# Moving the matmul operands of a two-layer encoder kernel to other SBUF addresses, with three more warming products

## The chip, the cores and the metric

The kernel runs on one core of a Trainium2 chip. The metric is the device time of one execution in microseconds. Before the change three runs gave 1088.2, 1091.89 and 1095.99 us, so the median is 1091.89 us. All times of single instructions below come from one profiled execution of its own.

## What is computed

The reference is a two-layer streaming encoder in float32, on 512 frames of width 1024. Cut to what matters here, one layer is:

```python
h = rms(x, norm1); z = h @ w_in            # 1024 -> 2572 columns, three groups of heads
x = x + concat(swa(z), fox(z), mlstm(z)) @ w_out      # 1024 -> 1024
u = rms(x, norm2) @ w_ff1                  # "first matrix", 1024 -> 4096
x = x + square(relu(u)) @ w_ff2            # "second matrix", 4096 -> 1024
```

`swa` is sliding-window attention with sinks and rotary positions, `fox` is attention with a forgetting bias, and `mlstm` is a chunkwise matrix memory. The change touches only the two products of the feed-forward part, `w_ff1` and `w_ff2`, and the first microseconds of the program.

## The kernel before

**Three products for one.** Every large matmul is done on float32r operands that are split into a high and a low part: `mm3` (lines 260 to 263) issues high times high (L261), high weight times low operand (L262) and low weight times high operand (L263), all three added in one PSUM bank. ScalarE rounds a weight tile to its high part `whi` (L203), VectorE subtracts to get the low part `wlo` (L204). Both are 128 x 1024 tiles with three buffers each. Weights arrive in `raw` and `fraw` tiles by DMA.

**Which side is loaded.** In the input projection (`big_work`, lines 516 to 552) the activations `xhl` are the stationary operand, loaded into the array 128 columns at a time, and `whi`/`wlo` stream through, 256 or 268 columns wide. In the output projection (L553 to L572) and in the feed-forward part the weights are stationary, and the activations stream: `yg` 512 columns wide in the output projection, `xhl` 512 columns wide in the first eight steps of the feed-forward part, then everything 256 columns wide. TensorE runs a weight load for the next matmul while the present one streams (PEld beside PE in the profile).

**The feed-forward part** (lines 1071 to 1335). The first quarter of the first matrix is done plainly (`ff1_std`), the rest of it and all of the second matrix with seven products in place of eight for each 2 x 2 block of sub-matrices (`ff1_st`, `ff2`; the order of the seven is ORDER, line 47). The seven products need sums and differences of blocks:

- The sums of x for the first matrix lie in the tile `xbx` (8 x 1024 floats a partition): `xsums` writes them, `xop` picks them (lines 332 to 370).
- The operands of the second matrix are sums of squared activations, made in the tile `ct` and split by `gsplit` and `csplit` (lines 1146 to 1155) into *units* of 1024 floats, which is 4096 bytes a partition. A unit holds the high or the low part of a pair of blocks (in `csplit` both, one block each). There are fourteen units in a queue, `units` (lines 1084 and 1085): six in the tile `gx`, eight in the tile `ygx`, which held the attention's output `yA` before. They are handed out by `unit_for` and given back by `give`. Two more, `quads`, lie in `xhl` and join late.

**Order of the work.** The generators of the first and the second matrix alternate by hand: `ff_pairs` (lines 117 to 126) gives the order, `getjob`/`prep_ahead` split weights up to three jobs ahead (`HIB`), and `load_ahead` starts DMAs as soon as a `raw` or `fraw` buffer is free.

**Addresses.** Tiles of one phase come from a pool that is opened with `open_phase` and gets the byte addresses from its tags in order of first use. In the program as compiled, the byte address inside a partition, taken modulo 512, is:

| operand | first address | modulo 512 | role |
|---|---|---|---|
| `whi`, `wlo` (all buffers) | 108992 ... 129472 | 448 | stationary in the output projection and feed-forward part, streaming in the input projection |
| `xhA`, `xlA` in `xhl` | 30720 | 0 | stationary, input projection |
| `yA` in `ygx` | 63936 | 448 | streaming, output projection |
| `xh`, `xl` in `xhl` | 30592 | 384 | streaming, feed-forward part |
| `xbx` (sums of x) | 134528 | 384 | streaming, first matrix |
| units 0 to 5 in `gx` | 167296 + 4096 i | 384 | streaming, second matrix |
| units 0 to 7 in `ygx` | 63872 + 4096 i | 384 | streaming, second matrix |

Every slice that a matmul streams or loads starts a multiple of 512 bytes after the tile or unit, so the last column but one holds for all of them. Before, a 40-float tile `pad` at the start of the feed-forward pool moves `xbx` and `gx` from 224 to 384 modulo 512.

**The start of the program.** Eight products of the constant tile `ones_m` with itself (lines 290 and 291) run while the first DMAs are under way. Each is a plain float32 matmul and has two records in the profile.

Of the kernel before, what the change touches and what calls it, by code (L numbers as in the profile page):

```python
# [13 lines left out]
F32R = mybir.dt.float32r  # L14
# [5 lines left out]
P = 128  # L20
D = 1024
S = 512
# [6 lines left out]
EPS = 1e-6  # L29
WGAP = 32  # L30
YGAP = 16
SWA_Q = 512
THETA = 10000.0

# [16 lines left out]
def trunk(ctx, tc, x, cols, rows, gate_w, tabs, w_in, w_out, w1, w2, out):  # L51
# [5 lines left out]
    xpool = ctx.enter_context(tc.tile_pool(name="xpool", bufs=1))  # L57
# [7 lines left out]
    def nm(s):  # L65
        cnt[0] += 1
        return f"{s}_{cnt[0]}"

    ATT = {"ms": (S, 5), "zq": (640, 6), "zv": (260, 8), "tmp": (768, 3), "rowb": (S, 4), "scs": (S, 4),
           "qk": (2 * S, 5), "pT": (S, 4), "hs": (256, 2), "co": (256, 4)}  # L70
    FFP = {"pad": (40, 1), "xbx": (8 * D, 1), "gx": (6 * D, 1), "xt": (S, 2), "ct": (6 * S, 1), "fraw": (4 * D, 1),
           "ms": (S, 2)}
    phase = {}

    def open_phase(tags):
        stack = ExitStack()
        phase["stack"] = stack
        phase["tags"] = tags
        phase["pool"] = stack.enter_context(tc.tile_pool(name=nm("ph"), bufs=1))

    def close_phase():
        phase.pop("stack").close()
        phase.clear()

    def wt(tag, name):
        n, bufs = phase["tags"][tag]
        return phase["pool"].tile([P, n], F32, tag=tag, name=nm(name), bufs=bufs)

    def att():
        return atp.tile([P, S], F32, tag="at", name=nm("at"))  # L90
# [4 lines left out]
    def v3(a, d=HD):  # L95
        return a.rearrange("p (h d) -> p h d", d=d)
# [175 lines left out]
    gx = cst.tile([P, NT, 36], F32, name="gx")  # L272
# [5 lines left out]
    XS = KT * S  # L278
    xT = xpool.tile([P, KT, S], F32, name="xT")
    xhl = xpool.tile([P, 2 * XS + 4 * WGAP], F32R, name="xhl")  # L280
    ygx = xpool.tile([P, 16 * S + YGAP], F32R, name="yg")
    sq_acc = {}
    xhA, xlA = (v3(xhl[:, WGAP + i * XS:WGAP + (i + 1) * XS], S) for i in range(2))
    xh, xl = (v3(xhl[:, i * XS:(i + 1) * XS], S) for i in range(2))
    yA, yg = v3(ygx[:, YGAP:], S), v3(ygx[:, :16 * S], S)


    open_phase(ATT)
    wps = att()
    for _ in range(8):  # L290
        T.matmul(wps[:, :P], ones_m, ones_m, start=True, stop=True)
    NN = 2 * L * KT
    pcol = cst.tile([P, NN + 2 * L], F32, name="pcol")
# [38 lines left out]
    def xb(i, j, t=None):  # L332
        t = (xh if t is None else t).rearrange("p (k i) q -> p k i q", i=2)
        return t[:, :, i, j * 256:(j + 1) * 256]
# [109 lines left out]
    for l in range(L):  # L444
# [612 lines left out]
        ct, bt = 0, 0  # L1057
# [13 lines left out]
        close_phase()  # L1071
        open_phase(FFP)
        pos["ff"] = l
        wt("pad", "pad")
        xbt["x"] = wt("xbx", "xbx").bitcast(F32R)
        gxt = wt("gx", "gx").bitcast(F32R)
        ct = v3(wt("ct", "ct"), S)
        fr = wt("fraw", "fraw")
        free_ff.extend(fr[:, i * D:(i + 1) * D] for i in range(4))
# [1 line left out]

        def unit(a):
            return a.rearrange("p (a f) q -> p a f q", a=2)
        units = deque(unit(v3(gxt[:, i * D:(i + 1) * D], 256)) for i in range(6))
        units.extend(yg[:, 2 * i:2 * i + 2].rearrange("p a (f q) -> p a f q", f=2) for i in range(8))
        quads = [unit(xb(0, 1, t_)) for t_ in (xh, xl)]
        banks = deque(att() for _ in range(8))

# [258 lines left out]
def _layout(x, norm1, w_in, swa_q_norm, swa_k_norm, swa_sinks, fox_q_norm, fox_k_norm, fox_f_bias, mlstm_i_bias,  # L1347
# [13 lines left out]
    def heads(w):  # L1361
        return w.reshape(2, 4, HD, -1).transpose(1, 0, 2, 3).reshape(SWA_Q, -1)
    w_in = cc([np.stack([heads(w[:, :SWA_Q].T).T for w in w_in]), w_in[:, :, SWA_Q:]], 2)
    w_out = cc([np.stack([heads(w[:SWA_Q]) for w in w_out]), w_out[:, SWA_Q:]], 1)
    cb = [np.stack([w_in[l][:, g[1][0][0]:g[1][0][0] + 256] for g in GROUPS]) for l in range(L)]
# [29 lines left out]
```

## Time and profile before

| | us |
|---|---|
| runs of the kernel | 1088.2, 1091.89, 1095.99 |
| profiled execution, device time | 1083.42 |
| profiled execution, span from first to last instruction | 1081.7 |
| TensorE with a matmul in it | 1064.2 |
| TensorE with a weight load in it | 997.5 |
| VectorE busy | 923.0 |
| ScalarE busy | 625.2 |

The stages of the profiled execution follow each other on TensorE: input projection of layer 0 from 6 us, with the attention's small matmuls between its products, output projection to 225 us, the 512-wide steps of the feed-forward part to 271 us, its 256-wide steps to 544 us; then the same for layer 1, from 544 to 686, 760, 806 and 1081.7 us.

How to read it: a matmul's record lasts from its start to a modelled end, some 280 ns for 256 columns, and the next one starts long before that end. So neither the mean of a group nor the busy share tells what a matmul costs. What it costs is the distance between the starts of neighbours, called *spacing* here. It comes from a table of stretches: the length of a stretch in which PE is busy throughout, divided by the matmuls in it, after taking off those that had started before the stretch (about 280 ns of records divided by the spacing).

### The profile page before, as it was taken

The page shows a single profiled execution, that of the slowest core. Times are in us where ns is not written, and L with a number is a line of the kernel's source. Part 1 is how long each engine was busy: PE and PEld are TensorE (multiplying, and loading weights), DVE is VectorE, ACT ScalarE, POOL GpSimd, SP SyncE. Part 2 cuts the span into 40 slices and gives each one's busy share as a digit, 9 for nine tenths or more (in the row PEclk, how much of TensorE's full clock was granted, in tenths as well). Part 3 has the DMA queues.
Part 4 walks back from the last instruction along what each step waited for, and adds up shares of the span by engine and source line. Part 5 has one row for each costly group of instructions (what it writes and reads, how often), then busy time and mean ns, then how long its engine had stood idle before and what let it go on. Part 6 is the DMA issues. An engine that isn't in the chain of part 4 may idle for free.

```text
span 1081.7 us, 21133 instructions
## 1 busy us (share of the span) xinstructions
PE 1064.2 (98%) x8488; PEld 997.5 (92%) x8488; DVE 923.0 (85%) x1572; ACT 625.2 (58%) x1099; POOL 106.3 (10%) x154
## 2 busy tenths in 40 slices
PE   9999999999999999999999999999999999999998
PEld 8999987887999999999999999778789999999998
DVE  7696868899997988999967877778999889899996
ACT  6445655375666667566545466544766575666552
POOL 2030010103110010010001200101000100010100
PEclk9999999999999999999999999999999999999999
DMA  6522111245378587587334321113334865876862
GB/s 216 161 95 97 60 59 58 65 169 127 115 201 218 132 218 209 145 211 210 106 110 158 96 78 55 65 50 128 114 91 137 233 176 169 240 177 174 221 171 98
DMA packets 47346, 151.81 MB, mean 140 GB/s; under 512 B 5632, under 2 KB 8832, under 8 KB 47248
## 3 DMA queue, kind: packets, MB, share of 16 engines
q1 hardware_dynamic: 39184, 121.10, 32.9%
q0 software_dynamic: 8064, 29.36, 15.5%
q8 instruction: 66, 1.08, 0.4%
q14 instruction: 32, 0.26, 0.1%
HBM read 147.86 MB, written 2.13 MB: 139 GB/s over the span
## 4 chain that ended last, share of the span: by engine, by line
PE 65%; DVE 18%; DMA 7%; ACT 6%; issue 3%; SPq 0%; POOL 0%; DVEq 0%; ACTq 0%; POOLq 0%
PE at L261 19%; PE at L263 19%; PE at L262 19%; DVE wlo L204 5%; DMA raw<-in_w_dram 5%; DVE rt L703 2%; DMA fraw<-in_w_dram 2%; ACT whi L203 2%; DVE xT L1257 1%; DVE yg L1150 1%; PE at L876 1%; PE at L834 1%; PE at L859 1%; PE at L733 1%; PE at L788 1%
## 5 line engine op out<-in xcount | busy, mean ns | idle before, releaser
L203 ACT ACTIVATE whi<-raw 128x1024 fp32r<-128x1024 f32 (+1 forms) x144 | 150.8, 1047 | 132.8 <-PE at L262 90.2
L204 DVE TENSOR_TENSOR wlo<-raw,whi 128x1024 fp32r<-128x1024 f32 (+1 forms) x144 | 174.7, 1213 | 38.4 <-ACT whi L203 37.8
L261 PE MATMUL at<-whi,xhl 128*128 128x256 f32 (+1 forms) x640 | 183.9, 287 | 1.2 <-ACT whi L203 1.2
L261 PE MATMUL at<-yg,whi 128*128 128x256 f32 (+1 forms) x592 | 180.1, 308 | 0.1
L262 PE MATMUL at<-wlo,xhl 128*128 128x256 f32 (+1 forms) x640 | 179.9, 281 | 0.1
L263 PE MATMUL at<-whi,xhl 128*128 128x256 f32 (+1 forms) x640 | 179.6, 281 | 0.0
L263 PE MATMUL at<-yg,wlo 128*128 128x256 f32 (+1 forms) x592 | 178.8, 302 | 0.5 <-DVE wlo L204 0.5
L203 ACT ACTIVATE whi<-fraw 128x1024 fp32r<-128x1024 f32 x122 | 129.3, 1060 | 85.0 <-PE at L262 67.2
L262 PE MATMUL at<-yg,whi 128*128 128x256 f32 (+1 forms) x560 | 169.7, 303 | 0.0
L262 PE MATMUL at<-xhl,whi 128*128 128x256 f32 (+1 forms) x544 | 165.5, 304 | 0.0
L204 DVE TENSOR_TENSOR wlo<-fraw,whi 128x1024 fp32r<-128x1024 f32 x122 | 148.9, 1221 | 6.1 <-ACT whi L203 5.6
L261 PE MATMUL at<-xhl,whi 128*128 128x256 f32 (+1 forms) x480 | 148.6, 310 | 0.0
L263 PE MATMUL at<-xhl,wlo 128*128 128x256 f32 (+1 forms) x480 | 147.8, 308 | 0.0
L261 PEld LDWEIGHTS at<-whi,xhl 128*128 128x128 f32 x640 | 121.4, 190 | 2.6 <-ACT whi L203 1.5
L262 PEld LDWEIGHTS at<-wlo,xhl 128*128 128x128 f32 x640 | 121.4, 190 | 0.4 <-DVE wlo L204 0.4
L263 PEld LDWEIGHTS at<-whi,xhl 128*128 128x128 f32 x640 | 121.4, 190 | 0.2 <-DVE xhl L328 0.2
L263 PEld LDWEIGHTS at<-yg,wlo 128*128 128x128 f32 x592 | 111.1, 188 | 6.2 <-DVE wlo L204 0.9
L261 PEld LDWEIGHTS at<-yg,whi 128*128 128x128 f32 x592 | 111.3, 188 | 5.9 <-issue 1.7
L263 PE MATMUL at<-xbx,wlo 128*128 128x256 f32 x384 | 106.6, 278 | 4.1 <-DVE wlo L204 4.1
L262 PEld LDWEIGHTS at<-yg,whi 128*128 128x128 f32 x560 | 105.3, 188 | 4.2 <-DVE yg L988 0.5
L262 PEld LDWEIGHTS at<-xhl,whi 128*128 128x128 f32 x544 | 102.1, 188 | 6.3 <-issue 0.5
L261 PE MATMUL at<-xbx,whi 128*128 128x256 f32 x384 | 106.3, 277 | 0.0
(284 smaller groups left out, 2436.7 us busy)
## 6 DMA issues: line engine op xcount, KB each, us to landing
fraw<-in_w_dram SPq DMA_DIRECT2D x90, 512.0 KB, 4.5
raw<-in_w_dram SPq DMA_DIRECT2D x66, 512.0 KB, 4.2
raw<-in_w_in_dram SPq DMA_DIRECT2D x34, 512.0 KB, 3.5
fraw<-in_w_dram POOLq DMA_DIRECT2D x34, 512.0 KB, 6.8
raw<-in_w_dram POOLq DMA_DIRECT2D x22, 512.0 KB, 7.9
raw<-in_w_out_dram SPq DMA_DIRECT2D x16, 512.0 KB, 3.3
rowb<-drow SPq DMA_DIRECT2D x16, 256.0 KB, 4.0
raw<-in_w_in_dram SPq DMA_DIRECT2D x12, 256.0 KB, 4.4
```

The lines of the kernel that those rows point to most:

```text
L203: A.activation(hi[:, cs_], raw[:, cs_], AF.Copy)
L204: V.tensor_tensor(lo[:, cs_], raw[:, cs_], hi[:, cs_], ALU.subtract)
L261: T.matmul(o, sh, mh, start=first, stop=False, skip_group_check=skip)
L262: T.matmul(o, sh, ml, start=False, stop=False, skip_group_check=skip)
L263: T.matmul(o, sl, mh, start=False, stop=last, skip_group_check=skip)
L703: V.tensor_tensor(r10[:, oo:oo + n, a:a + 32], z10[:, oo:oo + n, b:b + 32], tb(S_, n, a, a + 32), ALU.mult)
L733: T.matmul(sc[r][:, g * 256:g * 256 + nk], qTA[g][r * 64:(r + 1) * 64, c * P:(c + 1) * P], kTA[r * 64:(r + 1) * 64, k0:k0 + nk], start=Tru ...
L788: T.matmul(po[r * 64:(r + 1) * 64, g * P:(g + 1) * P], vt[:w, r * 64:(r + 1) * 64], p1[:w, u * P:(u + 1) * P], start=g == 0, stop=p2 is No ...
L834: T.matmul(sp[:, :nk], qTB[rs, pr, n * P:(n + 1) * P], kTB[rs, pr, :nk], start=True, stop=False)
L859: T.transpose(pt[:, b * P:(b + 1) * P], scs[r][:, b * P:(b + 1) * P], ident)
L876: T.matmul(pobs[pr][r * 64:(r + 1) * 64, n * P:(n + 1) * P], zbv[b][:, h * 64:(h + 1) * 64], ps[r][:, b * P:(b + 1) * P], start=b == 0, st ...
L1150: V.tensor_tensor(lo, c4(a, a + 2), hi, ALU.subtract)
```

## The change

- The units are 4128 bytes apart in place of 4096, both in `gx` and in `ygx`, so that each starts 32 bytes further on modulo 512 than the one before it. `ygx` grows by 128 floats (512 bytes) to hold them. `yA` stays where it is.
- In the feed-forward pool `gx` comes first and the tile `pad` is gone. Everything behind `ygx` moves up by 512 bytes, which is nothing modulo 512. So `gx` starts at 224 modulo 512, and `xbx` behind its 6 x 4128 bytes at 224 + 24768, which is 416 modulo 512. `ct`, `fraw` and `xt` move from 384 to 416 modulo 512 as well.
- The start runs eleven products of constants in place of eight.

The diff adds, removes and reshapes no other instruction and no DMA. After the change the units lie at these addresses modulo 512:

| tile | unit 0 | 1 | 2 | 3 | 4 | 5 | 6 | 7 |
|---|---|---|---|---|---|---|---|---|
| `gx` | 224 | 256 | 288 | 320 | 352 | 384 | | |
| `ygx` | 384 | 416 | 448 | 480 | 0 | 32 | 64 | 96 |

```diff
+UGAP = 8
...
-    FFP = {"pad": (40, 1), "xbx": (8 * D, 1), "gx": (6 * D, 1), "xt": (S, 2), "ct": (6 * S, 1), "fraw": (4 * D, 1),
+    UG = D + UGAP
+    FFP = {"gx": (6 * UG, 1), "xbx": (8 * D, 1), "xt": (S, 2), "ct": (6 * S, 1), "fraw": (4 * D, 1),
            "ms": (S, 2)}
...
-    ygx = xpool.tile([P, 16 * S + YGAP], F32R, name="yg")
+    ygx = xpool.tile([P, 16 * S + YGAP + 128], F32R, name="yg")
...
-    yA, yg = v3(ygx[:, YGAP:], S), v3(ygx[:, :16 * S], S)
+    yA = v3(ygx[:, YGAP:YGAP + 16 * S], S)
...
-    for _ in range(8):
+    for _ in range(11):
         T.matmul(wps[:, :P], ones_m, ones_m, start=True, stop=True)
...
-        wt("pad", "pad")
+        gxt = wt("gx", "gx").bitcast(F32R)
         xbt["x"] = wt("xbx", "xbx").bitcast(F32R)
-        gxt = wt("gx", "gx").bitcast(F32R)
...
-        units = deque(unit(v3(gxt[:, i * D:(i + 1) * D], 256)) for i in range(6))
-        units.extend(yg[:, 2 * i:2 * i + 2].rearrange("p a (f q) -> p a f q", f=2) for i in range(8))
+        units = deque(unit(v3(gxt[:, i * UG:i * UG + D], 256)) for i in range(6))
+        units.extend(unit(v3(ygx[:, i * UG:i * UG + D], 256)) for i in range(8))
```

## The prediction

> **What bounds the kernel now.** I read the page first: busy times, then the chain that ended last.
>
> ```profile
> span 1081.7 us, 21133 instructions
> ...
> PE 1064.2 (98%) x8488; PEld 997.5 (92%) x8488; DVE 923.0 (85%) x1572; ACT 625.2 (58%) x1099; POOL 106.3 (10%) x154
> ...
> PE 65%; DVE 18%; DMA 7%; ACT 6%; issue 3%; SPq 0%; POOL 0%; DVEq 0%; ACTq 0%; POOLq 0%
> ```
>
> TensorE nearly always has a matmul under way, and weight loads fill 92% of the span, more than any other engine's work. So I ask at what spacing the matmuls start. The next view is the table of stretches: two long ones inside the 256-wide feed-forward steps, one of the input projection of layer 1, one of the 512-wide feed-forward steps, one of the output projection. The columns are the stretch, its length, then busy time and count of PE, PEld, DVE, ACT and POOL.
>
> ```profile
> 285.00:430.00 145.00, 145.00 (x1282) 145.00 (x1281) 126.38 (x135) 93.29 (x112) 13.85 (x16) 1.00 0.73 198
> 900.00:1035.00 135.00, 135.00 (x1194) 135.00 (x1193) 124.77 (x139) 85.81 (x103) 12.14 (x14) 1.00 0.74 200
> 544.50:555.50 11.00, 11.00 (x96) 11.00 (x95) 8.72 (x18) 6.01 (x11) 0.53 (x1) 1.00 0.31 97
> 226.00:247.00 21.00, 21.00 (x92) 16.85 (x91) 20.77 (x35) 14.18 (x23) 1.01 (x1) 1.00 0.29 88
> 205.30:213.80 8.50, 8.50 (x39) 7.04 (x38) 7.08 (x15) 1.81 (x4) 1.17 (x4) 1.00 0.37 123
> ```
>
> Some 2.4 matmuls of 256 columns (1.7 of 512) had started before a stretch and come off its count. The feed-forward spacing is 145/1279.6 = 113.3 ns, and 135/1191.6 = 113.3 ns in the other layer: a matmul every 113.3 ns, with no idle time for 145 us. In the third row it is 11/93.6 = 117.5 ns for the same width. The fourth gives 21/90.3 = 233 ns for 512 columns, the fifth 8.5/37.3 = 228 ns.
>
> So in the part that the change touches the kernel is bound by TensorE's own rate, not by data. The other two engines have room there (DVE 126 of 145 us, ACT 93), and a change is worth the number of matmuls times what it does to their spacing.
>
> What sets 113.3? Six matmuls of the gate computation load full 128 x 128 weights, but stream only 24 to 8 columns:
>
> ```profile
> 38.74 0.81 PE L630 MATMUL at<-gate,ones_m 128*128 128x24 f32 x6
> 39.41 0.37 PE L261 MATMUL at<-whi,xhl 128*128 128x256 f32 x1
> ```
>
> From the first of the six to the matmul behind them are 0.67 us: 0.67/6 = 111.7 ns each, with almost nothing streamed. A weight load alone takes that long, so I read 111.7 as the floor and the other 1.6 ns as what streaming and loading cost each other.
>
> **Which matmuls change address.** The groups by line and shape, columns: count, busy time, mean of one record.
>
> ```profile
> L263 PE MATMUL at<-yg,wlo 128*128 128x256 f32 x464 | 128.5, 277 | 0.5 <-DVE wlo L204 0.5
> L261 PE MATMUL at<-yg,whi 128*128 128x256 f32 x464 | 128.5, 277 | 0.1
> L262 PE MATMUL at<-yg,whi 128*128 128x256 f32 x432 | 119.4, 276 | 0.0
> ...
> L263 PE MATMUL at<-xbx,wlo 128*128 128x256 f32 x384 | 106.6, 278 | 4.1 <-DVE wlo L204 4.1
> L261 PE MATMUL at<-xbx,whi 128*128 128x256 f32 x384 | 106.3, 277 | 0.0
> L262 PE MATMUL at<-xbx,whi 128*128 128x256 f32 x384 | 106.2, 277 | 0.0
> L263 PE MATMUL at<-gx,wlo 128*128 128x256 f32 x368 | 102.0, 277 | 1.9 <-DVE wlo L204 1.9
> L261 PE MATMUL at<-gx,whi 128*128 128x256 f32 x368 | 102.0, 277 | 0.9 <-ACT whi L203 0.9
> ...
> L262 PE MATMUL at<-gx,whi 128*128 128x256 f32 x336 | 92.9, 277 | 0.0
> ```
>
> Sums of x: 3 x 384 = 1152. Units: 464 + 464 + 432 + 368 + 368 + 336 = 2432, some 174 for each of the fourteen; two units stay at 384, so 2084 of them move. That is 3236 matmuls; one nanosecond of spacing on all of them is 3.2 us, 0.3% of the run.
>
> **What an address costs.** Call *offset* the streamed operand's address minus that of the weights, modulo 512. Before, it is -64 in every 256-wide matmul of the feed-forward part, in the input projection and in the 512-wide steps, and 0 in the output projection. Rows of the stretches show that this region matters and that the offset is not all of it. At 512 columns, 0 is better than -64 by 233 - 228 = 5 ns. At 256 columns and -64, the same offset gives 113.3 ns in one place and 117.5 in another, so it also depends on how far the load runs ahead of the stream, and a dense run of matmuls keeps the beat it has.
>
> After the change xbx is at -32. The units run over -224 ... -64 and -64 ... +160 in steps of 32. The trace has no 256-wide matmul there, so I bound the cost: not below the floor, -1.6 ns; not above the slower beat, 117.5 - 113.3 = +4.2 ns. For an offset of 0 I take the floor, since the row of 0 saves 2.5 ns per 256 columns and the floor allows 1.6. For -32 and +32, between or beside known offsets, half of that, 0.8. For the nine other units no row is near; between two far ends I take the nearest in kind, the feed-forward's own 113.3, thus 0.
>
> - xbx: 1152 x -0.8 ns = -0.9 us (bounds -1.8 and +4.8).
> - The units at 416, 448 and 480: 174 x -(0.8 + 1.6 + 0.8) ns = -0.6 us, and 0 for nine units. Bounds for all twelve: 2084 x -1.6 ns = -3.3 us and 2084 x 4.2 ns = +8.8 us.
>
> **VectorE and ScalarE** read and write the moved tiles too. Their rows do not see the address modulo 512:
>
> ```profile
> L204 DVE TENSOR_TENSOR wlo<-raw,whi 128x1024 fp32r<-128x1024 f32 x140 | 171.9, 1228 | 35.8 <-ACT whi L203 35.3
> L204 DVE TENSOR_TENSOR wlo<-fraw,whi 128x1024 fp32r<-128x1024 f32 x122 | 148.9, 1221 | 6.1 <-ACT whi L203 5.6
> ...
> L1150 DVE TENSOR_TENSOR yg<-ct,yg 128x1024 fp32r<-128x1024 f32 x14 | 16.9, 1219 | 0.0
> ```
>
> Sources at equal addresses modulo 512 (raw and whi; ct and yg) take 1228 and 1219 ns, sources 64 bytes apart (fraw and whi) 1221. I cost it at nothing; its cover is the 13% of those stretches in which DVE is idle.
>
> **The new order in the pool** puts gx where the squares of layer 1's input (L322) come to lie in layer 0's wake, so these must now wait for the last read of a unit.
>
> ```profile
> 544.12 0.28 PE L263 MATMUL at<-gx,wlo 128*128 128x256 f32 x1
> ...
> 544.91 1.13 ACT L322 ACTIVATE sq<-xT 128x512 f32<-128x512 f32 x2
> ```
>
> That read ends at 544.40, and the first square starts at 544.91 anyway. Nothing queues behind it on ACT, and I cost it at 0.
>
> **Three more warming products.** The first rows of the timeline:
>
> ```profile
> 1.12 3.78 PE L291 MATMUL at<-ones_m 128*128 128x128 f32 x16 [1.12 <-DVE zc L270]
> ...
> 6.15 0.58 PE L261 MATMUL at<-whi,xhl 128*128 128x256 f32 x1 [1.25 <-ACT whi L203]
> ...
> 6.88 0.58 PE L262 MATMUL at<-wlo,xhl 128*128 128x256 f32 x1
> ...
> 8.88 0.75 DVE L328 SCALAR_TENSOR_TENSOR xhl<-xT,pcol,xhl 128x512 fp32r<-128x512 f32 x1
> ...
> 9.39 0.42 PE L261 MATMUL at<-whi,xhl 128*128 128x256 f32 x1
> ...
> 9.60 0.42 PE L262 MATMUL at<-wlo,xhl 128*128 128x256 f32 x1
> 9.68 0.29 PEld L263 LDWEIGHTS at<-whi,xhl 128*128 128x128 f32 x1
> ...
> 10.67 0.28 PE L261 MATMUL at<-whi,xhl 128*128 128x256 f32 x1
> ...
> 10.79 0.28 PE L262 MATMUL at<-wlo,xhl 128*128 128x256 f32 x1
> ```
>
> ```profile
> L263 PEld LDWEIGHTS at<-whi,xhl 128*128 128x128 f32 x640 | 121.4, 190 | 0.2 <-DVE xhl L328 0.2
> ```
>
> The matmuls start 0.21 us apart at 9.39 and 9.60 and 0.12 apart at 10.67 and 10.79: until 10.67 the array ran at half rate. The sixteen records end at 4.90 and the first real product starts at 6.15, when whi is there. Six more records at (3.78 - 0.42)/15 = 0.22 us are 1.3 us; they end near 6.2 but leave the array at 6.0 (a record outlasts its slot by 0.2), so they delay nothing. If the full rate comes earlier, little is gained before 9.68: that load waits (last row, the only such wait of its group) for the low part of the second block of x, written by DVE until 8.88 + 0.75 = 9.63, and before it the array would only wait longer. From 9.68 to 10.67 at double rate is a gain of 0.5 us; if the rate rises no earlier, 0. I take -0.5.
>
> The Trainium skill, "TensorE: Matmul & The Clock Gate", Part 1 (The HAM clock gate), says that the gate watches free-running windows of 3.4 us and opens after one sustained busy one. By that rule the gain hangs on where a window falls: counted back from the rise at 10.67, one runs from 7.25 and one from 3.84, and the second would still hold part of the wait before the product at 6.88, so the sum might lose its 0.5 us here. The trace neither shows the windows nor excludes them.
>
> **The sum.** -0.9 - 0.6 - 0.5 = -2.0 us. Made against the profiled execution: 1083.4 (span 1081.7 and 1.7 around it) becomes 1081.4. That execution lies 8.5 us under the median of the runs, which themselves spread over 7.8. Against the median the forecast is 1091.9 - 2.0 = 1089.9 us.
>
> **The rivals.**
>
> 1. *The floor is reached.* Spread offsets take streaming and loading out of each other's way: 3236 x -1.6 - 0.5 = -5.7 us, 1086.2. For it: the 111.7 of the gate matmuls. Against it: 117.5 at an unchanged offset shows more than the offset at work.
> 2. *The slower beat*, on the other side. High and low units now have different offsets, so between L261, L262 and L263 the stream jumps against the load, and the run falls into the beat of 117.5: 3236 x 4.2 = +13.6 us, 1105.5. For it: the third row of stretches. Against it: 145 us without one lapse before. It makes a loss of 1% (10.9 us) once 80% of the moved matmuls are caught.
> 3. *Addresses do not count.* 113.3 is the array's own cost of a pair of load and stream: only the start gains, 1091.4. For it: all three families have means of 276 to 278 ns and share one spacing. Against it: 228 and 233 at 512 columns. The Trainium skill, "SBUF — State Buffer", section "Who interferes with whom", speaks for this rival: PE has two independent read ports, one for the streamed operand and one for weight loads, and never waits on anyone. The trace does not agree at 512 columns, by those 5 ns.
> 4. *More than the floor allows.* At half rate 256 columns took 0.21 us, half of which is 106 ns, 7 ns under 113.3: 3236 x 7 = -23 us, 1069. Against it: the 111.7 of a load alone.
>
> **How the numbers follow.** Forecast 0.45, with 1087 to 1094 as its own range; rival 1 0.16; rival 2 0.14, of which 0.11 past 1%; rival 3 0.17; rival 4 0.08. A measurement of this kernel tells about 1%, 10.9 us, from no change. Faster by more than that is rival 4 alone, 0.08; slower 0.11; within it 0.81. The range runs from 1081, rival 1 less the runs' scatter of some 5 us, to 1105, nearly all of rival 2.
>
> **What would show it.** In the changed profile the stretches 285 to 430 and 900 to 1035 should hold 3 to 8 matmuls more (spacing 112.6 to 113.2). Spacing at 111.7 means rival 1, above 114.5 rival 2, 113.3 unchanged rival 3, under 111 rival 4. The full rate should come before 10.67 us, while the load that waits for the second block of x still starts near 9.7. DVE's L204 should stay within 1215 to 1235 ns. The prediction is wrong if the spacing of xbx and of the units moves apart by more than 2 ns, or if the time comes from another stage.

## The result and the profile after

The changed kernel takes 1097.9 us (median of 13 runs, 1096.1 to 1099.3), the kernel before 1090.8 us in the runs beside them (13 runs, 1085.4 to 1096.0). The ratio is 1.0072, with a 95% interval of 1.0053 to 1.0091: slower by 0.7%, 7.1 us of medians, where 2.0 us less were forecast. Note that the runs after spread over 3 us and those before over 11.

The page of the profile after, as far as it answers to the rows shown of before:

```profile
span 1096.0 us, 21145 instructions
...
PE 1083.0 (99%) x8494; PEld 1017.3 (93%) x8494; DVE 926.2 (85%) x1572; ACT 626.2 (57%) x1099; POOL 106.7 (10%) x154
...
PE 77%; DVE 15%; ACT 5%; issue 2%; DMA 1%; SPq 0%; DVEq 0%; ACTq 0%
```

The span grew by 14.3 us, TensorE's busy time by 18.8, and DVE, ACT and POOL did the same work in nearly the same time. In the chain that ended last TensorE itself rose from 65% to 77%, and DMA went from 7% to 1%: the kernel now waits less for anybody and is longer all the same.

Where the time went shows when the stages are cut at the same instructions. First the 256-wide feed-forward steps of both layers before, then after (columns as in the prediction's table of stretches):

```profile
271.10:544.20 273.10, 268.49 (x2353) 267.29 (x2352) 249.40 (x276) 169.06 (x201) 23.00 (x27) 1.00 0.65 176
806.30:1081.70 275.40, 268.41 (x2353) 267.01 (x2351) 243.64 (x268) 163.12 (x192) 21.64 (x25) 1.00 0.64 176
```

```profile
270.70:551.80 281.10, 278.91 (x2353) 278.25 (x2352) 251.41 (x276) 169.85 (x201) 23.08 (x27) 0.99 0.64 171
813.40:1096.00 282.60, 277.65 (x2353) 276.79 (x2351) 245.13 (x268) 163.54 (x192) 21.64 (x25) 1.00 0.64 172
```

The same 2353 matmuls take 8.0 us more in layer 0 and 7.2 us more in layer 1. That is 15.2 us, more than the whole 14.3; the other stages together are 0.9 us shorter. And the stretches of the forecast, with two stages that the change leaves alone:

```profile
285.00:430.00 145.00, 145.00 (x1232) 145.00 (x1232) 122.04 (x130) 88.29 (x106) 12.99 (x15) 1.00 0.71 190
900.00:1035.00 135.00, 135.00 (x1151) 135.00 (x1151) 121.12 (x131) 81.67 (x97) 12.13 (x14) 1.00 0.70 188
226.00:247.00 21.00, 21.00 (x91) 16.84 (x90) 20.81 (x35) 13.94 (x24) 1.01 (x1) 1.00 0.30 92
205.30:213.80 8.50, 8.50 (x40) 6.99 (x39) 7.08 (x15) 1.74 (x5) 1.17 (x4) 1.00 0.39 123
```

The first two hold 50 and 43 matmuls less than before. The spacing is 145/1229.6 = 117.9 ns and 135/1148.6 = 117.5 ns, where it was 113.3, at a granted clock of 1.00. That is above the 114.5 at which the prediction's rival 2 begins. The 512-wide stretches did not move.

The records of single matmuls, put beside the program's addresses, give the spacing of each operand (mean distance to the next start, waits left out):

| operand | offset | before | after |
|---|---|---|---|
| `xbx` | -64 before, -32 after | 113.5 | 118.3 |
| units moved | -64 before, twelve others after | 113.4 | 117.7 to 119.1 |
| units 5 of `gx` and 0 of `ygx` | -64 in both | 113.4 | 115.9 and 116.7 |
| `xhl`, 256-wide | -64 in both | 113.4 | 116.1 |

Every offset but -64 is near 118, and operands that did not move at all became slower too. Summed over the operands: 1152 x 4.8 + 2115 x 4.85 + 1120 x 2.7 + 302 x 2.9 ns = 19.7 us. (In all 2128 matmuls of moved units; the prediction's even split of the units gave 2084.) The distances over 150 ns, which are TensorE's waits and a dip of its clock, sum to 4.6 us less than before (6.3 for 10.9), which leaves 15.1 of the 15.2 us.

TensorE's waits, whole execution, after and then before:

```profile
PE at L265 <- DVE wlo L206: 2.7, 4, 1.8
PE at L712 <- DVE z L707: 2.1, 2, 1.1
```

```profile
PE at L263 <- DVE wlo L204: 6.5, 8, 2.0
PE at L261 <- ACT whi L203: 2.1, 3, 1.2
```

The waits for split weights fall from 8.6 us to 2.7: a TensorE that takes longer for a job gives ScalarE and VectorE longer for the next one.

### The profile page after: what moved, and what is told of

It reads as the page before. It is cut to its first block, busy times and chain, and to the rows that moved or that the text cites. A ratio compares the mean times of both kernels' runs of the same rounds, so it can differ in the third digit from the quotient of the medians.

```text
span 1096.0 us, 21145 instructions
## 1 busy us (share of the span) xinstructions
PE 1083.0 (99%) x8494; PEld 1017.3 (93%) x8494; DVE 926.2 (85%) x1572; ACT 626.2 (57%) x1099; POOL 106.7 (10%) x154
## 4 chain that ended last, share of the span: by engine, by line
PE 77%; DVE 15%; ACT 5%; issue 2%; DMA 1%; SPq 0%; DVEq 0%; ACTq 0%
PE at L263 23%; PE at L265 23%; PE at L264 23%; DVE wlo L206 4%; DVE rt L705 2%; ACT whi L205 1%; DVE xT L1258 1%; PE at L735 1%; PE at L790 1%; PE at L878 1%; DVE yg L1151 1%; DVE z L701 1%; DVE z L707 1%; PE at L794 1%; ACT pe L748 1%
## 5 line engine op out<-in xcount | busy, mean ns | idle before, releaser
L206 DVE TENSOR_TENSOR wlo<-raw,whi 128x1024 fp32r<-128x1024 f32 (+1 forms) x144 | 174.8, 1214 | 39.7 <-ACT whi L205 39.4
L263 PE MATMUL at<-yg,whi 128*128 128x256 f32 (+1 forms) x592 | 181.9, 311 | 0.0
L264 PE MATMUL at<-yg,whi 128*128 128x256 f32 (+1 forms) x560 | 171.5, 306 | 0.0
L206 DVE TENSOR_TENSOR wlo<-fraw,whi 128x1024 fp32r<-128x1024 f32 x122 | 149.2, 1223 | 11.6 <-ACT whi L205 11.2
L263 PEld LDWEIGHTS at<-yg,whi 128*128 128x128 f32 x592 | 111.7, 189 | 5.5 <-issue 1.7
L263 PE MATMUL at<-xbx,whi 128*128 128x256 f32 x384 | 108.5, 282 | 0.0
L264 PE MATMUL at<-xbx,whi 128*128 128x256 f32 x384 | 108.4, 282 | 0.0
```

Source lines behind the costliest of these rows:

```text
L206: V.tensor_tensor(lo[:, cs_], raw[:, cs_], hi[:, cs_], ALU.subtract)
L263: T.matmul(o, sh, mh, start=first, stop=False, skip_group_check=skip)
L264: T.matmul(o, sh, ml, start=False, stop=False, skip_group_check=skip)
```

## The experiments

Three theories for the 118 ns:

- **A**: each offset has its own price, and -64 happens to be the cheap one.
- **B** (the prediction's rival 2 as it was written): an offset costs nothing by itself; what costs is that the stream jumps against the load from one matmul to the next.
- **C**: at the same offset there are two beats, 113.3 and some 118 ns. A stall or a disturbance decides which one the following matmuls keep. Before's profile was then an execution that happened to be nearly always in the first one.

### Before once more, the warming alone, the sums alone, the units alone

`again` is the kernel before, unchanged. `warm` has eleven warming products and nothing else. `sums` and `units` are one half each of the move of addresses:

```diff
 sums:
-    FFP = {"pad": (40, 1), "xbx": (8 * D, 1), "gx": (6 * D, 1), ...
+    FFP = {"pad": (40, 1), "gx": (6 * D, 1), "pad2": (8, 1), "xbx": (8 * D, 1), ...
 units: the change, with
-    for _ in range(11):
+    for _ in range(8):
-    FFP = {"gx": (6 * UG, 1), "xbx": (8 * D, 1), ...
+    FFP = {"gx": (6 * UG - UGAP, 1), "xbx": (8 * D, 1), ...
```

> The kernel before, unchanged, profiled once more. Theory A (the offset of each streamed operand from the weights sets its own spacing, -64 is the cheap one) and theory B (what costs is a change of the offset from one matmul to the next; any constant offset is cheap) both expect 113.3 ns in the 256-wide feed-forward steps and about 1083 us of span, and leave open why the runs lie at a median of 1091. Theory C (at a constant offset of -64 there are two beats, 113.3 and 117.8 ns, and which one a stretch falls into is left to chance) expects other stretches than in the first profile to be at 117 to 118 ns, a span up to 10 us longer, and runs that scatter over 10 us.

> Eleven products of constants, addresses as before. All theories: the full rate comes at 6 to 8 us in place of 10.7, the gain is at most 0.5 us, ratio 0.998 to 1.002, and the feed-forward spacing is that of the kernel before.

> The sums of x alone at 416 modulo 512, all units and the eight products at the start as before. Theory A: 1152 matmuls at 118.3 ns in place of 113.3, the others unchanged: +5.8 us on the profile with the fast beat throughout. Theory B: only the jumps between groups of 24 matmuls count: inside a group of sums the spacing comes back to 113.3, and the whole costs under 2 us. Theory C: the sums at 118 ns, and the neighbours at -64 thrown into the slower beat too, up to +4 us more.

> The units 4128 bytes apart as in the change, the sums of x kept at 384, eight products at the start. Theory A: 2084 moved matmuls at +5 ns, the rest unchanged: +10 us against a profile of the kernel before at 113.3 throughout. Theory B: the same or less, since high and low units of a pair differ by 32 bytes and each L264-like product jumps; the two units at 384 suffer too. Theory C: the units at 118, and the sums and xhl, though at -64, at 116 to 118 as well: +14 us or more.

| kernel | median us (lowest to highest) | ratio to before, 95% |
|---|---|---|
| `again` | 1089.5 (1082.5 to 1091.7) | 0.9997 (0.9971 to 1.0022) |
| `warm` | 1088.6 (1083.2 to 1092.2) | 0.9997 (0.9970 to 1.0024) |
| `sums` | 1089.6 (1088.0 to 1091.8) | 1.0010 (0.9992 to 1.0028) |
| `units` | 1095.7 (1094.2 to 1097.2) | 1.0076 (1.0048 to 1.0103) |

The units carry the loss; the warming carries nothing that can be measured. Now the same two stretches of `warm`, whose addresses are those of before, and a stretch of layer 1 of `again`:

```profile
285.00:430.00 145.00, 145.00 (x1281) 144.98 (x1280) 127.07 (x137) 92.94 (x112) 13.87 (x16) 1.00 0.73 199
900.00:1035.00 135.00, 135.00 (x1149) 135.00 (x1148) 121.12 (x134) 82.83 (x99) 12.17 (x14) 1.00 0.70 195
```

```profile
947.20:1057.20 110.00, 110.00 (x936) 110.00 (x935) 104.49 (x120) 68.17 (x81) 10.44 (x12) 1.00 0.73 189
```

145/1278.6 = 113.4 ns in layer 0 and 135/1146.6 = 117.7 ns in layer 1: the same program text, the same addresses, the same full clock, no wait, and two beats. That misses the expectation for `warm`, which was the spacing of before in both. The slower stretch begins behind a wait at 890.6 us and ends at one at 1055.9. In `again` one (110/933.6 = 117.8 ns) begins behind waits at 944 to 947 us and lasts to the end, and its 256-wide steps of layer 1 take 276.9 us to the last matmul, where before's profile has 271.3. That is theory C. In the feed-forward steps of before, `again`, `warm` and `sums_192` (below) every change from one beat to the other lies at a wait or at a dip of the clock, though many waits change nothing. Theory C also says what before's profile was: 1083.4 us, near the lowest of its many runs (1082.1 to 1098.8 in all the comparisons).

`sums` speaks against B. Both halves of each sum lie at -32, so nothing jumps within a product of 24 matmuls, and yet these have a spacing of 118.1 ns to their last one, while the operands at -64 around them return to means of 113.6 to 114.7. A change of offset isn't quite free all the same: the first five matmuls at -64 behind a sum have 118 to 123 ns. The stretches of `sums` lie between the two beats, 145/1259.6 = 115.1 and 135/1173.6 = 115.0 ns:

```profile
285.00:430.00 145.00, 145.00 (x1262) 145.00 (x1261) 125.79 (x134) 91.19 (x110) 13.88 (x16) 1.00 0.72 197
900.00:1035.00 135.00, 135.00 (x1176) 135.00 (x1175) 123.36 (x136) 84.54 (x101) 11.95 (x14) 1.00 0.71 195
```

In `units` the moved units have 117.6 to 119.3 ns, and `xbx`, at -64 as before, 116.1: products at -64 between products at other offsets often stay in the slower beat. Its profiled run is 12.4 us longer than before's, between the 10 of A and the 14 of C.

### Products alone

`micro1` and `micro2` hold no encoder: 128 x 128 weights, 256 streamed columns, three products as in `mm3`, in runs of 72 and 48. A product is a single matmul in these tests.

> No encoder at all, its output is zeros: runs of 72 products in the three-term pattern of the feed-forward steps, 256 columns wide, each after a pause and at one offset, for 19 offsets from -256 to +224 bytes, and for -64 also with the weights 32, 64 and 256 bytes further on; each four times: straight after the pause, after one and after two products of 512 columns, and after a float32 product of 24 columns. Theory A with C: at -64 a run has 113.3 or 117.8 ns, by how it starts; at every other offset that the change used (-224 to -96, -32 to +160) 118 to 119 ns however it starts; the same with the weights moved, since only the difference counts. Theory B: every constant offset comes to 113.3. A third view, that the address itself and not the difference counts, expects the runs with moved weights to differ from -64 at the first place.

> No encoder, output zeros: again runs of products 256 columns wide. (a) Offsets -76 to -52 in steps of 4 bytes, four starts each: if the fast beat needs the offset exactly, all lie at 117 to 120 ns; if it has a width, -68 and -60 show 113.3 at times or always. (b) Sixteen runs at -64 after a pause: by chance, some 5 to 11 of the 16 at 113.3, the rest at 117.8. (c) High operand at -64 and low at +192: theory A, with the period of 256 bytes, expects 113.3 or 117.8 as at -64, though the stream jumps; theory B expects neither to hold. High at -64 and low at -32 or 0: 116 to 118 by A. (d) Runs of 24 at -64 with 1, 2, 4 or 8 triples at another offset between them: if a stretch at another offset throws the dice again, the runs behind it are a mixture; if it leads into the fast beat, all are at 113.3.

Four pieces of `micro1`, each from the start of one matmul to the start of the fortieth behind it (two of the 42 had started before): at -64, at -64 from another start, at -32 and at 0.

```profile
290.14:294.67 4.53, 4.53 (x42) 4.53 (x41) 0.00 (x0) 0.00 (x0) 0.00 (x0) 1.00 0.01 4
299.71:304.42 4.71, 4.71 (x42) 4.71 (x41) 0.00 (x0) 0.00 (x0) 0.00 (x0) 1.00 0.00 0
367.81:372.54 4.73, 4.73 (x42) 4.73 (x41) 0.00 (x0) 0.00 (x0) 0.00 (x0) 1.00 0.00 0
445.87:450.67 4.80, 4.80 (x42) 4.80 (x41) 0.00 (x0) 0.00 (x0) 0.00 (x0) 1.00 0.00 0
```

That is 113.3, 117.8, 118.3 and 120.0 ns. No other engine is at work in them, so none of them makes the difference. Spacing in ns at all offsets, second part of each run. Offset modulo 256, since -256 and 0, -224 and +32 and so on gave the same:

| offset | -128 | -96 | -80 | -76 to -52, without -64 | -64 | -48 | -32 | -16 | 0 | +32 | +64 | +96 |
|---|---|---|---|---|---|---|---|---|---|---|---|---|
| ns | 119 to 120 | 117 to 119 | 119.3 | 117.5 to 123.5 | 113.3 or 117.8 | 119.1 | 118.3 | 117.2 | 120.0 | 116.6 to 117.8 | 117.8 | 120 |

Moving the weights and the stream together by 32, 64 or 256 bytes gave the same values, but for one start of four at -32, which had 120.0: the difference counts. The 113.3 ns exist at exactly -64 (or +192), four bytes to either side they are gone, and at -64 they are a matter of the start: 13 of 16 equal runs had 113.3 and three 117.8. The start moves some other offsets too, but by less: 116.7 or 117.8 at +32, 118.6 or 120.0 at -128, 117.3 or 118.7 at -96.

High parts at -64 with low parts at +192 gave 113.3 in four of four, so a distance of 256 bytes costs nothing; by that period the two are one offset, and the pair tests no other jump. What puts B out as the cause is the table: constant offsets have no jump and cost 117 to 120 ns. Whether a jump costs something besides is open. High at -64 with low at -32 gave 119.1, above the 118.3 of -32 alone; high at -32 with low at -64 gave 117.7, and high at -64 with low at 0 gave 117.8 to 119.5. A and C are both true: A for every offset but one, with that small effect of the start, and C for that one, where the start makes 4.5 ns.

`micro2` also had stretches of 24 products at -64 with a few at another offset between them. With 3, 6, 12 and 24 at -32 between them, five, one, four and none of eight stretches ran at 117.8; with three at 0 the first two did, with three at -16 or +32 none.

### Everything at offset 0, and the sums 256 bytes away

`all_0` puts every stream of the feed-forward part at 448 modulo 512, the address of the weights. `sums_192` puts `xbx` at +192, which the products alone say is the same as -64.

```diff
 all_0:
-    FFP = {"pad": (40, 1), ...
+    FFP = {"pad": (56, 1), ...
-    xh, xl = (v3(xhl[:, i * XS:(i + 1) * XS], S) for i in range(2))
-    yA, yg = v3(ygx[:, YGAP:], S), v3(ygx[:, :16 * S], S)
+    xh, xl = (v3(xhl[:, 16 + i * XS:16 + (i + 1) * XS], S) for i in range(2))
+    yA, yg = v3(ygx[:, YGAP:], S), v3(ygx[:, 16:16 + 16 * S], S)
 sums_192: as sums, with
-    "pad2": (8, 1)
+    "pad2": (64, 1)
```

> Every streamed operand of the feed-forward part at 448 modulo 512, so at the constant offset 0; nothing jumps. Theory B (only jumps cost): 113.3 ns throughout, median 1083 or less since the 512-wide steps gain 5 ns each (384 of them, 2 us). Theory A: 117.8 ns in all 4704 products of 256 columns, +21 us on a profile at 113.3 throughout, about 1100 us in the runs, less 2 us for the 512-wide steps.

> As the kernel with the sums of x alone moved, but to 128 modulo 512, which is offset +192. Theory A with the period of 256 bytes found in the products by themselves: the sums at 113.3 or 117.8 ns like everything at -64, no groups of 118.3, median as before (1085 to 1092). Theory B, that a change of offset between groups costs: as with the sums at 416.

`all_0` takes 1107.0 us (1105.6 to 1107.8), ratio 1.0143 (1.0109 to 1.0177). Nothing jumps in it, and its stretches are the slowest of all: 145/1206.6 = 120.2 ns and 135/1124.6 = 120.0 ns. A had expected 117.8 and about 1100 us.

```profile
285.00:430.00 145.00, 145.00 (x1209) 145.00 (x1208) 119.53 (x127) 85.80 (x103) 12.98 (x15) 1.00 0.69 186
900.00:1035.00 135.00, 135.00 (x1127) 135.00 (x1127) 119.43 (x129) 81.69 (x98) 11.25 (x13) 1.00 0.65 175
226.00:247.00 21.00, 21.00 (x94) 17.41 (x93) 20.93 (x36) 14.53 (x23) 1.01 (x1) 1.00 0.28 87
```

Its third row is the 512-wide steps, at offset 0 too: 94 matmuls in place of 92. So 0 is better than -64 for 512 columns, as the prediction read from before, and the stage takes 44.4 us in place of 45.7. For 256 columns it is 6.7 ns worse.

`sums_192` takes 1089.1 us (1084.9 to 1097.1), ratio 0.9987 (0.9956 to 1.0018): no difference, as a period of 256 bytes has it. Its profiled execution, 1095.2 us of span, fell into the slower beat at 285.7 us, at the end of a dip of its clock, and left it at a wait at 526.4:

```profile
285.00:430.00 145.00, 145.00 (x1231) 145.00 (x1231) 121.51 (x129) 87.50 (x105) 12.99 (x15) 1.00 0.70 190
```

145/1228.6 = 118.0 ns for all operands alike, at the offset of before. One execution at the good offset can thus be as long as one of the changed kernel (this one has two dips of the clock as well, of some 1.3 us each).

### Ending the slower beat

If the beat at -64 is kept until something disturbs it, a few products at another offset might end the slower one. `micro3` tries six such *resets*, with three products at -32 between them, which throw most stretches into the slower beat.

> Products alone, 128 x 128 weights under 256 streamed columns; the encoder is left out and the output is zeros. Four blocks of the same row for each of six resets: 24 products at offset -64, three products at -32 (which in the run before left 113.3 and 117.8 ns taking turns), 24 at -64, the reset, and again, four times over. Resets: three products at -16, at +32, at -128, and 24 products at the same three offsets. Theory C (two beats at -64, kept until something disturbs them; some offsets end the slower one): after the switch at -32 half of the stretches run at 117.8, after 24 products at +32 or -16 all are back at 113.3, and after three products at -16 or +32 as well if the offset and not the length matters. Rival: a disturbance merely draws lots again, so that stretches after each reset are at 117.8 in 20 to 50% of the cases, whatever its offset and length; then no cheap reset exists.

| reset | stretches at 117.8 before it, of which at 113.3 behind it |
|---|---|
| 3 products at +32 | 16 of 16 |
| 24 products at +32 | 8 of 8 |
| 3 products at -16 | 12 of 16, the last of each row not |
| 24 products at -16 | 0 of 8 |
| 3 products at -128 | 16 of 16 |
| 24 products at -128 | 8 of 8 |

After 24 products at +32 or -16, stretches that had been at 113.3 stayed there (8 of 8 each); after 24 at -128 they fell to 117.8 (8 of 8). The four rows of a reset are nearly alike. So it is no lottery: what follows hangs on the state before, the offset and the number of products and, as three at -16 show at the end of a row, on something more; and +32 brought the better beat in every case. The rival is out; the expectation for 24 products at -16 failed.

`reset` builds this into the kernel before: the first of the four slices of each sum of x lies at +32, by its own gap of 40 floats (the former `pad`), the rest at -64. `reset_warm` has eleven warming products as well.

```diff
-    FFP = {"pad": (40, 1), "xbx": (8 * D, 1), "gx": (6 * D, 1), ...
+    FFP = {"xbx": (8 * D + 40, 1), "gx": (6 * D, 1), ...
+    def xb4(n):
+        t = xbt["x"]
+        def sl(k):
+            at = k * 2048 + n * 256 + (40 if k else 0)
+            return t[:, at:at + 256]
...
-        wt("pad", "pad")
```

> Before, with one change of addresses: of the four slices of each sum of x, the first lies at offset +32 modulo 256 and the others stay at -64. So 6 of the 24 matmuls of each product of a sum, 288 in all, serve as a reset. Theory C with the measured reset (after +32 every stretch at -64 ran at 113.3 ns): the 6 cost 3.4 to 4.5 ns each, 1.0 to 1.3 us in all; from the second quarter of each feed-forward part on no stretch at 117.8 lasts longer than to the next sum of x, some four products of 24; the 256-wide steps take 273 to 275 us in each layer, and the runs lie at 1082 to 1088 with a median near 1085, 0.3 to 0.6% below before. Rival (each disturbance draws lots): stretches at 117.8 come as often as before or more often, median 1090 to 1095.

> The same addresses and eleven warming products in place of eight. By theory C the same feed-forward part, and 0 to 0.5 us less at the start: median 1084 to 1085, under the kernel before and far under the changed one (1097.9). By the rival 1089 to 1095, no better than before.

`reset` takes 1086.9 us (1085.4 to 1090.0), ratio 0.9988 (0.9965 to 1.0012); `reset_warm` 1087.6 us (1084.7 to 1089.9), ratio 0.9991 (0.9967 to 1.0014). Every run of both lies at least 6 us under every run of the changed kernel. Against before the medians are 2.4 and 1.7 us lower, which the intervals do not tell from nothing. The scatter fell from 12.4 us (22 of the 23 runs beside them; the longest, 1098.8, left out) to 4.6 and 5.1, at both ends: the lucky executions at 1082 are gone as well.

```profile
320.00:430.00 110.00, 110.00 (x969) 110.00 (x969) 95.61 (x102) 69.73 (x85) 10.39 (x12) 1.00 0.75 205
```

110/966.6 = 113.8 ns in layer 0. The 6 matmuls at +32 have 117.7 ns, 4.3 more than 113.4, so all 288 cost 1.2 us. But the reset is not certain in the kernel. After a wait of some 2.2 us in the midst of a sum's first matmuls eight groups of 24 matmuls ran at 117.8 ns; the next sum of x did not end that, only the one after it did. The last 209 matmuls of layer 1, behind waits and with no sum among them, ran at 117.8 as well. `reset_warm` has both in its layer 1. Six products at +32 are a number that `micro3` did not try. Part of the expectation failed there; the median came out 2 us above the forecast 1085.

## Why the prediction was wrong

**The bound was right.** TensorE's spacing sets these steps, and the loss is matmuls times nanoseconds. `xbx` and the moved units stayed together, both near 118.3 ns, and the time came from the stage that was named.

**The step that failed is the costing of the offsets**: for 0 "I take the floor" (-1.6 ns), "for -32 and +32 ... half of that", "for the nine other units ... I take the nearest in kind, the feed-forward's own 113.3, thus 0". Measured against 113.3 in the changed kernel: +5.0 ns for `xbx` at -32, +5.1 for the unit at +32, +4.4 for the unit at 0 (whose partner lies elsewhere; with high and low both at 0 it is +6.7), +4.6 to +5.8 for the others. Two inferences led there. The 5 ns by which 0 beats -64 at 512 columns were carried over to 256 columns; both are true, `all_0` shows them in one execution, but with opposite signs. And 113.3 was taken for the ordinary cost of a pair of load and stream, with 111.7 as a floor that other offsets might come nearer to. It is the exception: of all the offsets tried only -64 modulo 256 reaches it, and not always. No run went clearly below it towards the floor, which was read from plain float32 matmuls and not from float32r ones. The nearest row in kind was the wrong choice there; the far end of the bounds, 117.5, is close to what all but one of the offsets have.

**The upper bound was a little short.** -1.6 to +4.2 ns were given; the moved operands came out 4.4 to 5.8 ns up.

**Rival 2 had the price and not the mechanism.** It gave +13.6 us through the beat of 117.5; the profiles differ by 14.3. That it comes so close is luck in part: it was set against the median, 1105.5 us, and there it is 7.6 us too high. And no jump between high and low is needed: the sums of `sums` and everything in `all_0` have none and are slow. "145 us without one lapse", the argument against it, was one execution; `again`, `warm` and `sums_192` lapse for 136 to 241 us on end at the same offset.

**The remark that 113.3 and 117.5 occur at one offset** was the right clue, and was put down to how far the load runs ahead. It is theory C, seen in the input projection: of its 256-wide matmuls in before's trace some 1090 have a distance of 112 to 115 ns and some 510 one of 116 to 119. The forecast treated that as a property of the place and not as a state that the feed-forward part of another execution may be in as well.

**The base.** The sum was made against 1083.4 us, an execution almost wholly in the better beat, and then moved to the median. The same +15 us count fully only against such an execution. The runs of before already hold slower stretches: (1090.8 - 1.7 - 1081.7)/4.4 ns is some 1700 of the 4704 matmuls, over a third, in an average run (an estimate from the medians and the two beats, which neglects the waits). The profiled executions of before, `again`, `warm` and `sums_192`, whose operands all lie at -64 modulo 256, have some 2, 27, 30 and 60% of them there. By this estimate it accounts for profiles that differ by 14.3 us and medians that differ by 7.1, and for the small scatter of the runs after: they have hardly any better beat to lose.

**Rival 3** had on its side a rule of the Trainium skill, "SBUF — State Buffer", section "Who interferes with whom": PE reads the stream and the weights by two independent ports and never waits on anyone. These runs do not agree: with everything else equal the distance of the two addresses makes 113.3, 117.8 or 120.0 ns. Where in the chip that arises is not shown.

**VectorE, ScalarE and the order in the pool** cost nothing, as said. L206, the former L204:

```profile
L206 DVE TENSOR_TENSOR wlo<-raw,whi 128x1024 fp32r<-128x1024 f32 x140 | 172.1, 1229 | 37.7 <-ACT whi L205 37.3
L206 DVE TENSOR_TENSOR wlo<-fraw,whi 128x1024 fp32r<-128x1024 f32 x122 | 149.2, 1223 | 11.6 <-ACT whi L205 11.2
```

**The warming** was mis-sized. The timeline of the start after:

```profile
1.12 5.07 PE L293 MATMUL at<-ones_m 128*128 128x128 f32 x22 [1.12 <-DVE zc L272]
5.84 0.56 PE L263 MATMUL at<-whi,xhl 128*128 128x256 f32 x1
6.48 0.38 PE L264 MATMUL at<-wlo,xhl 128*128 128x256 f32 x1
6.70 0.28 PE L265 MATMUL at<-whi,xhl 128*128 128x256 f32 x1
...
7.72 0.28 PE L265 MATMUL at<-whi,xhl 128*128 128x256 f32 x1
8.59 0.38 PE L263 MATMUL at<-whi,xhl 128*128 128x256 f32 x1 [0.59 <-ACT xhl L329]
8.81 0.28 PE L264 MATMUL at<-wlo,xhl 128*128 128x256 f32 x1
9.38 0.39 PE L265 MATMUL at<-whi,xhl 128*128 128x256 f32 x1 [0.29 <-DVE xhl L330]
```

The full rate came at 6.3 us and, as forecast, was spent on waiting: the matmul that needs the second block of x starts at 9.38, behind a wait for that block (9.81 before). The output projection begins 0.2 us earlier than before, not 0.5, and the first real product had already started 0.3 us earlier. And the credit is not the warming's: with eight products the full rate came at 10.6 us in before, at 5.2 in `units` and `reset`, 5.3 in `sums`, 5.4 in `all_0`, 12.5 in `sums_192` and 4.3 in `again` (where it was lost from 7.7 to 11.2), with eleven at 5.6 in `warm` and at 4.9 in `reset_warm`, where it was lost again from 11.7 to 15.1.

## What to carry to other kernels

Before moving an operand that a dense run of matmuls streams, look at its address minus that of the weights loaded beside it, modulo 256, and measure the offset by itself at the width in use: here one single offset was, in its better beat, 3 to 10 ns a matmul better than all others tried at 256 columns, and 0 and -64 changed places at 512. When the runs of an unchanged kernel scatter by 1% and its profile lies at their lower end, look for stretches of equal work in other executions before taking the profile's spacing as the kernel's own. A forecast made from one execution in the better of two states has to be set against the median with the states' shares, not with a constant added.

## What the runs showed of the hardware

- At 256 float32r columns over a 128 x 128 load the spacing hangs on the difference of the two addresses modulo 256 bytes: 120.0 ns at 0, 117 to 120 nearly everywhere, and 113.3 or 117.8 at exactly -64. Once in one of the two, a run without waits kept it, in `sums_192` for 241 us.
- With products alone, a few at another offset change the state in a repeatable way (three at -32 mostly took 113.3 to 117.8, three or 24 at +32 always gave back 113.3); in the kernel six at +32 ended the slower state at one sum of x and not at another. What inside the chip holds this state is not shown by any of these runs.
- The clock fell to half for 3.4 us after a wait of some 2 us in the midst of a dense stage, in some executions and not in others. After has one, at 282.8 us:

```profile
279.00:282.50 3.50, 1.71 (x15) 1.51 (x14) 3.50 (x5) 2.00 (x2) 0.00 (x0) 1.00 0.00 0
282.80:286.20 3.40, 3.40 (x18) 3.40 (x17) 2.69 (x3) 0.70 (x1) 0.00 (x0) 0.50 0.75 254
286.20:290.00 3.80, 3.80 (x34) 3.80 (x33) 3.37 (x4) 1.91 (x3) 0.87 (x1) 1.00 0.67 125
```

The 18 matmuls of the second row would take 2.1 us at the spacing around them, so the dip costs 1.3 us at least; `all_0`, `sums_192` and `reset_warm` have one near the same place, before has the same wait and none. The Trainium skill, "TensorE: Matmul & The Clock Gate", Part 1 (The HAM clock gate), has free-running windows of 3.4 us, which agrees with the length of the dip; it lets the clock fall after an idle window, and here the window ahead of the dip was idle for about half.
